# Second pass of the attention scores: low part of k on both halves, 128 rows instead of 64

## The chip, the cores and the metric

One core of a Trainium2 chip runs the whole forward pass of a two-layer decoder trunk in one launch. The metric is device time in microseconds. The kernel before took 1227.51 us (median of 3 runs, 1226.98 to 1227.97). Five engines work side by side, each through its own queue in order: TensorE (PE in the profile, its weight loads PEld), VectorE (DVE), ScalarE (ACT), GpSimd (POOL) and SyncE (SP, which here issues the DMAs).

## The reference, cut to what matters

Sequence 512, width 1024, two layers. Each layer multiplies the normed input by one weight matrix whose columns are q, k, v and two branches of a recurrent block. The attention has 4 heads, and each head has two components of 64 dimensions:

```
s = einsum('bqhcd,bkhcd->bhcqk', q_blk, k) * scale      # c: two components, d: 64
s = where(causal mask, s, -inf)
pr = softmax(s)
attn = pr[:, :, 0] - lam * pr[:, :, 1]
out = attn @ v
```

After it come a norm of each head, the recurrent block (convolution, gates, scan), one output projection, an MLP with squared ReLU, and a gated embedding per layer. All is float32.

## The kernel before

Every tensor lies with features on the 128 partitions and the 512 tokens along the columns. TensorE multiplies in a format that keeps fewer bits than float32, so each operand is split into a high part (rounded by a ScalarE copy) and a low part (what is left, by a VectorE subtraction). A product of two tensors is then three passes: high by high, high by low, low by high. The weights come in chunks of 128x1024 by DMA (`raw`) and are split into `wh` and `wl`.

The two components of a head share one tile of 128 rows, 64 rows each. `rope_done` rotates q or k (it ends in `t1`) and splits it. For q it makes one tile per component, `x0` and `x1`: on the component's own 64 rows the high part, on the other 64 rows the low part. For k it makes `y0` and `y1`, the high part of a component on both halves, and one tile `lo` that holds the low part of component 0 in rows 0 to 63 and of component 1 in rows 64 to 127.

`unit_scores` then needs three passes for a block of 128 queries and one component, into one PSUM bank:

- the first has `q[c]` as stationary operand and `k[c]` as moving one, all 128 rows: high by high on one half, low by high on the other, summed in one pass;
- the second takes the high part of q and the low part of k, on the component's own 64 rows alone;
- the third adds the causal mask to the last 128 columns, an identity times a mask tile (`identr`, `maskr`), 128 rows.

Block qi has (qi + 1) x 128 columns, so the passes are 128, 256, 384 or 512 columns wide. There are 4 blocks x 2 components x 4 heads x 2 layers = 64 such triples. `unit_max` takes the maxima and exponentials, `unit_mix` mixes the two components, `unit_T` transposes and `head_av` multiplies by v.

All instructions are recorded first, through an object (`Plan`) that stands in for the engines. A list scheduler then sets the order of every engine at once: it takes what is ready by its own costs, oldest first with some boosts, within a window of 600 instructions. So dense products of the next head stand between the passes of a head's scores. Tiles of 128x512 come from one pool of 57 (`T`), score banks from 6 PSUM banks (`PM`), of which scores hold 4 at most. The profile puts every instruction on line 182, the line that issues them, so the tiles' names tell them apart: `sc` is a score bank, `ky` the high part of k, `kl` its low part, `qx` a q tile, `dense` the bank of a projection, `up` of the MLP's first product.

Of the kernel before, what the change touches and what calls it, by code (L numbers as in the profile page):

```python
# [21 lines left out]
KD = D // 128  # L22
# [3 lines left out]
NQ = KF // KD  # L26
ORDER = (0, 4, 1, 5, 2, 6, 3, 7)     # output tiles, so that the halves of the features that Strassen pairs come together
HS = S // 2
# [4 lines left out]

# buffers
TB = 57     # tiles of [128, 512]
AT = 2      # tiles for the probabilities of a head, transposed
RAW = 4     # weight chunks as loaded
WB = 6      # weight chunks, split
SC = 4      # PSUM banks that scores may hold

# chunks split ahead in the MLP's products
UA = 2
DA = 2

# the list schedule
WIN = 600   # instructions beyond the oldest one not issued that it may choose from
EV = 150    # boost of what frees PSUM
LP = 600    # how far the norm's sums are put off
RE = -50    # boost of the rotary tables
SW = 2      # us that an instruction waits at most for others that need no new activation table  # L50
SF = 8      # free tiles from which on no check for deadlock is needed
WU = 8      # products that warm up the tensor engine
NM = 4      # output tile of the first up product after which the norm's scale is computed

# [11 lines left out]
class Plan:  # L66
    """Records instructions and issues them in the order of a list schedule: each engine takes, of what is ready,
    what was recorded first (less its boost)."""

# [114 lines left out]
    def schedule(self):  # L184
# [36 lines left out]
        def safe(i):  # L221
            """Whether all that is older than the newest instruction issued can still find its tiles in program order."""
            need = {}
# [132 lines left out]

# columns of the packed per-feature vectors
VCOL = {}
# [16 lines left out]
def chunk_list():  # L375
    """Weight chunks of [128, 1024] in the order in which they are used."""
    c = []
    for l in range(DEPTH):
        c += [("in", l, 12 + m) for m in range(2)]
        c += [("gates", l, 0)]  # L380
        c += [("in", l, 12 + m) for m in range(2, 4)]
        c += [("v", l, i) for i in range(4)]
        for h in range(NH):
            c += [("in", l, h), ("in", l, 4 + h)]
        c += [("in", l, 16 + m) for m in range(4)]
        c += [("out", l, m) for m in ORDER]
        for q in range(NQ):
            c += [("up", l, q * KD + m) for m in range(KD)]
            c += [("down", l, m, q) for m in ORDER]
        c += [("proj", l, 0)]  # L390
        c += [("gate", l, m) for m in range(4)]
        c += [("proj", l, 1)]
        c += [("gate", l, m) for m in range(4, 8)]
    return c
# [6 lines left out]
def build(ctx: ExitStack, tc: tile.TileContext, given, x, p, pos, w, vec, lamqk, out):  # L401
# [25 lines left out]

    # ---------------- weights: streamed, split into two parts that add up exactly
    raw_t, w_t = {}, {}
# [3 lines left out]
    def w_half(i, c):  # L433
        """Half a chunk, for the products that come first."""
        t, hi, lo = T("w0"), T("w0h", F32R), T("w0l", F32R)
# [30 lines left out]
    def pair_parts(a1, a2):  # L466
        """The seven weight operands of Strassen's product (Winograd's form) for two output tiles."""
        lft, rgt = slice(0, S), slice(S, 2 * S)
# [37 lines left out]
    def split(src, hi, lo):  # L506
        """src (SBUF or PSUM) into hi + lo."""
        act(out=hi, in_=src, func=AF.Copy)
        ve.tensor_tensor(out=lo, in0=src, in1=hi.bitcast(F32), op=ALU.subtract)
# [8 lines left out]

    # ---------------- constants
    vt = const.tile([128, NV], F32, name="vt")  # L520
# [21 lines left out]
    def warm_up():  # L542
        """Products of zeros that bring the tensor engine to its full clock while the first loads run."""
        z = T("z", F32R)
# [15 lines left out]
    def rope_setup():  # L560
        """cos and signed sin of the angles, feature-major, 1 and 0 on the rows that don't rotate."""
        posf = T("posf")[:, 0:NT]
# [6 lines left out]
        NA = NT * 16  # L569
        # ang = hi + lo, 1/(2 pi) as a sum of 12-bit parts: every product is exact  # L570
        rest, parts = 1.0 / (2.0 * math.pi), []
# [58 lines left out]
    def vec_setup():  # L630
        for l in range(DEPTH):
            act(out=hb[:, l, 0:4], in_=vt[:, VCOL["b_gate_a", l]:VCOL["b_gate_a", l] + 4], func=AF.Copy, scale=0.5)
            act(out=hb[:, l, 4:8], in_=vt[:, VCOL["b_gate_x", l]:VCOL["b_gate_x", l] + 4], func=AF.Copy, scale=0.5)
            act(out=gsub[:, l:l + 1], in_=V("g_subln", l), func=AF.Copy, scale=1.0 - lam_init(l))
        # softplus(-x) = max(-x, 0) + log1p(exp(-|x|)), the log1p as 2 atanh(y / (2 + y))
        n = DEPTH * 4
# [18 lines left out]
        ve.tensor_scalar(out=sp4n.rearrange("p l t -> p (l t)"), in0=s, scalar1=-4.0, scalar2=None, op0=ALU.mult)  # L655
        # lambda of the differential attention, on every partition
        lq = T("lq")
# [11 lines left out]

    # ---------------- norms: h times its gain goes into the products, 1/rms after them  # L670
    class Norm:
# [20 lines left out]
        def stats(self, square=False):  # L692
            """1/rms (or its square), token-major, and spread over the partitions."""
            ps = PS("msq")
# [24 lines left out]
    class FinalNorm:  # L719
        """The last norm, on each half of the tokens as soon as that is complete."""  # L720

# [35 lines left out]
    def group(ws, rhs, nk, done, late=0, mid=None, tk=slice(0, S)):  # L757
        """ws: per output tile a function giving the chunk slices of K tile k. The last `late` K tiles come last."""
        pss_ = [PM("dense") for _ in ws]
# [16 lines left out]

    # ---------------- one layer
    def layer(l, h, nm, last):
        hg = lambda k: nm.hg[k]
        gate_w = [None]  # L780
        scan_o = [None] * 4
        yo = [None] * KD     # 0..3 attention heads, 4..7 recurrent tiles

# [4 lines left out]

        # recurrent branch
        lru = [dict() for _ in range(4)]  # L790
# [68 lines left out]

        # x branch  # L860
        ws = [take_in(12), take_in(13)]
# [8 lines left out]

        # v, token-major
        pv = [PM("pv") for _ in range(NT)]
# [19 lines left out]

        # attention
        mask_sh = [(i ^ 8) if i < 16 else i for i in range(32)]

        def rope_done(ps, dst):
# [6 lines left out]
            if not dst:  # L903
                # q: per component, its hi part on its own rows and its lo part on the other's
                x0, x1 = T("qx", F32R), T("qx", F32R)
# [5 lines left out]
            else:  # L911
                # k: per component, its hi part on both, and its lo part on its own rows
                y0, y1, lo = T("ky", F32R), T("ky", F32R), T("kl", F32R)
                for y, src in ((y0, t1[ca, :]), (y1, t1[cb, :])):
                    act(out=y[ca, :], in_=src, func=AF.Copy)
                    act(out=y[cb, :], in_=src, func=AF.Copy)
                for y, c in ((y0, ca), (y1, cb)):
                    ve.tensor_tensor(out=lo[c, :], in0=t1[c, :], in1=y[c, :].bitcast(F32), op=ALU.subtract)
                dst.append((y0, y1, lo))

        att, s0_ = {}, {}

        def unit_scores(hd, qi, q, k):
# [4 lines left out]
            for c in range(2):  # L928
                pc = slice(64 * c, 64 * c + 64)
                ps = PM("sc")  # L930
                mm(ps[:, 0:n], lhsT=q[c][:, qs], rhs=k[c][:, 0:n], start=True, stop=False)
                mm(ps[:, 0:n], lhsT=q[c][pc, qs], rhs=k[2][pc, 0:n], start=False, stop=False)
                mm(ps[:, qs], lhsT=identr, rhs=maskr, start=False, stop=True)
# [95 lines left out]

        # gate branch  # L1030
        for t in range(4):
            group([take_in(16 + t)], hg, KD, lambda i, ps: gr_done(t, ps))

        # output projection; the recurrent tiles come first, the last head last
        order = [4, 5, 6, 7, 0, 1, 2, 3]

        nm2 = Norm("g_mlp", l)
        bp = [dict() for _ in range(4)]     # Strassen's operands of h times its gain, per pair of feature tiles
        fp, t4s = [None] * KD, []
        fat = [AT, []]  # L1040

        def BT(name):
            """512 columns of a tile like those that hold a head's probabilities, as long as there are any."""
            if not fat[1] and fat[0]:
# [40 lines left out]

        # MLP in quarters of the hidden features; the first product by Strassen's method over pairs of output tiles,
        # halves of the input features and halves of the tokens
        nm3 = Norm("g_ple", l)
# [73 lines left out]

        # per-layer embedding
        nmn = None if last else Norm("g_mix", l + 1)
# [18 lines left out]
        def ple(ms, ws, tk, done, **kw):  # L1183
            """proj and gate products of the output tiles ms on the tokens tk."""
            pj = []
# [93 lines left out]
def _layout(i):  # L1279
    """Lays the arrays out as the launch reads them."""  # L1280
    a = {k: np.asarray(v) for k, v in i.items()}
# [59 lines left out]
```

## Time and profile before

| what | value |
|---|---|
| median of 3 runs | 1227.51 us |
| span of the profiled execution | 1225.4 us |
| PE busy | 1210.8 us (99%) |
| PEld busy | 1049.7 us (86%) |
| DVE busy | 949.0 us (77%) |
| ACT busy | 654.8 us (53%) |
| POOL busy | 21.4 us (2%) |
| mean DMA rate | 94 GB/s |

The span runs from the first to the last instruction of the execution that was profiled; the time of a run holds a little more than that. Busy times of an engine are unions of its instructions' durations. Those of PE overlap, since a product starts before the one ahead has drained: the distance between two starts tells what a pass costs the stream, and its duration is longer.

### The profile page before, as it was taken

To read this page: it belongs to the slowest core of one execution; us is meant where nothing else is said; L and a number is where in the kernel's file an instruction comes from. 1 tells how busy PE (TensorE), PEld (TensorE's weight loads), DVE (VectorE), ACT (ScalarE), POOL (GpSimd) and SP (SyncE) were. 2 spreads that over 40 slices of the span, in tenths; PEclk is the share of its full clock that TensorE was granted. 3 is DMA by queue.
4 is the path that set the end of the run, shared out by engine and by line. 5 is a ranking of instruction groups with operands and counts; after the bars stand their busy time and mean duration, and the time that the engine had idled before them with its cause. 6 is when DMAs were issued, how large, how long until landed. Compare 5 with 4: busy or idle time off the path is not lost.

```text
span 1225.4 us, 17658 instructions
## 1 busy us (share of the span) xinstructions
PE 1210.8 (99%) x6848; PEld 1049.7 (86%) x6848; DVE 949.0 (77%) x1642; ACT 654.8 (53%) x1068; POOL 21.4 (2%) x43
## 2 busy tenths in 40 slices
PE   8999999999999999999999999999999999999996
PEld 6877788998988989988888777889899899898886
DVE  9898889987777678575778888799776787786564
ACT  6875557743543535543458566576445354355352
POOL 1000000000000000000000000000000000000000
PEclk9999999999999999999999999999999999999998
DMA  6321133243332333332323111223433333343202
GB/s 234 103 69 52 52 89 101 85 124 100 106 103 90 118 93 114 103 103 87 104 69 118 55 35 52 75 81 107 134 103 104 91 104 97 91 136 103 86 1 69
DMA packets 34371, 114.71 MB, mean 94 GB/s; under 512 B 3952, under 2 KB 6000, under 8 KB 34288
## 3 DMA queue, kind: packets, MB, share of 16 engines
q1 hardware_dynamic: 34288, 113.59, 30.2%
q8 instruction: 54, 0.88, 0.3%
q14 instruction: 29, 0.24, 0.1%
HBM read 111.48 MB, written 2.10 MB: 93 GB/s over the span
## 4 chain that ended last, share of the span: by engine, by line
PE 94%; DVE 3%; ACT 1%; DMA 0%; issue 0%; POOL 0%; SPq 0%; POOLq 0%; DVEq 0%; ACTq 0%
PE dense L182 55%; PE up L182 26%; PE sc L182 4%; PE pv L182 2%; PE pj L182 2%; PE av L182 1%; PE bc L182 1%; PE tr L182 1%; PE msq L182 1%; PE osm L182 0%; PE gates L182 0%; DMA h<-x 0%; DVE hs L182 0%; DVE a L182 0%; ACT ky L182 0%
## 5 line engine op out<-in xcount | busy, mean ns | idle before, releaser
L182 ACT ACTIVATE wh<-raw 128x1024 fp32r<-128x1024 f32 x204 | 214.3, 1057 | 279.6 <-PE dense L182 151.8
L182 DVE TENSOR_TENSOR wl<-raw,wh 128x1024 fp32r<-128x1024 f32 x204 | 247.6, 1218 | 22.4 <-ACT wh L182 22.0
L182 PE MATMUL dense<-ffh,wh 128*128 128x512 f32 x512 | 199.5, 390 | 0.0
L182 PE MATMUL dense<-ffl,wh 128*128 128x512 f32 x512 | 199.4, 389 | 0.0
L182 PE MATMUL dense<-ffh,wl 128*128 128x512 f32 x512 | 199.2, 389 | 0.0
L182 PE MATMUL dense<-hgh,wl 128*128 128x512 f32 (+1 forms) x400 | 151.3, 378 | 0.0
L182 PE MATMUL dense<-hgh,wh 128*128 128x512 f32 (+1 forms) x400 | 151.1, 378 | 0.0
L182 PE MATMUL dense<-hgl,wh 128*128 128x512 f32 (+1 forms) x400 | 150.3, 376 | 0.0
L182 PEld LDWEIGHTS dense<-ffh,wl 128*128 128x128 f32 x512 | 96.1, 188 | 20.0
L182 PEld LDWEIGHTS dense<-ffh,wh 128*128 128x128 f32 x512 | 96.1, 188 | 19.8
L182 PEld LDWEIGHTS dense<-ffl,wh 128*128 128x128 f32 x512 | 96.2, 188 | 19.5
L182 ACT ACTIVATE sh<-s 128x512 fp32r<-128x512 f32 x96 | 59.9, 628 | 78.1 <-DVE s L182 77.6
L182 DVE TENSOR_TENSOR dn<-dense,rbc 128x512 f32<-128x512 f32 x64 | 44.2, 690 | 72.7 <-PE dense L182 71.9
L182 PE MATMUL up<-bl,wh 128*128 128x256 f32 x352 | 99.6, 283 | 0.0
L182 PE MATMUL up<-bh,wl 128*128 128x256 f32 x352 | 99.6, 283 | 0.0
L182 PE MATMUL up<-bh,wh 128*128 128x256 f32 x352 | 99.5, 283 | 0.0
L182 PEld LDWEIGHTS dense<-hgl,wh 128*128 128x128 f32 x400 | 75.5, 189 | 12.1
L182 PEld LDWEIGHTS dense<-hgh,wl 128*128 128x128 f32 x400 | 75.5, 189 | 11.9
L182 PEld LDWEIGHTS dense<-hgh,wh 128*128 128x128 f32 x400 | 75.5, 189 | 11.8
L182 PE MATMUL up<-bl,sh 128*128 128x256 f32 x288 | 81.5, 283 | 0.0
L182 PE MATMUL up<-bh,sl 128*128 128x256 f32 x288 | 81.5, 283 | 0.0
L182 PE MATMUL up<-bh,sh 128*128 128x256 f32 x288 | 81.3, 283 | 0.0
(236 smaller groups left out, 2572.0 us busy)
## 6 DMA issues: line engine op xcount, KB each, us to landing
raw<-w SPq DMA_DIRECT2D x204, 512.0 KB, 3.6
h<-x SPq DMA_DIRECT2D x8, 256.0 KB, 5.4
out<-fin SPq DMA_DIRECT2D x8, 256.0 KB, 2.4
w<-w SPq DMA_DIRECT2D x4, 256.0 KB, 4.5
pT<-p SPq DMA_DIRECT2D x4, 256.0 KB, 4.0
lq<-lamqk SPq DMA_DIRECT2D x1, 256.0 KB, 7.1
vt<-vec SPq DMA_DIRECT2D x1, 61.0 KB, 2.4
posi<-pos SPq DMA_DIRECT2D x1, 2.0 KB, 3.0
```

The lines of the kernel that those rows point to most:

```text
L182: d["fn"](*d["args"], **d["kw"])
```

## The change

For k, each component now has a low tile of its own, `los[0]` and `los[1]`. The subtraction writes the component's own half as before, and a ScalarE copy writes the same values into the other half. The second pass of the scores uses all 128 rows of `q[c]` and of that tile. It so adds the low part of q times the low part of k, which was left out before.

```diff
             else:
-                # k: per component, its hi part on both, and its lo part on its own rows
-                y0, y1, lo = T("ky", F32R), T("ky", F32R), T("kl", F32R)
-                for y, src in ((y0, t1[ca, :]), (y1, t1[cb, :])):
+
+                ys, los = [T("ky", F32R), T("ky", F32R)], [T("kl", F32R), T("kl", F32R)]
+                for y, src in zip(ys, (t1[ca, :], t1[cb, :])):
                     act(out=y[ca, :], in_=src, func=AF.Copy)
                     act(out=y[cb, :], in_=src, func=AF.Copy)
-                for y, c in ((y0, ca), (y1, cb)):
+                for y, lo, c, o in zip(ys, los, (ca, cb), (cb, ca)):
                     ve.tensor_tensor(out=lo[c, :], in0=t1[c, :], in1=y[c, :].bitcast(F32), op=ALU.subtract)
-                dst.append((y0, y1, lo))
+                    act(out=lo[o, :], in_=lo[c, :].bitcast(F32), func=AF.Copy)
+                dst.append((ys, los))
...
             for c in range(2):
-                pc = slice(64 * c, 64 * c + 64)
                 ps = PM("sc")
-                mm(ps[:, 0:n], lhsT=q[c][:, qs], rhs=k[c][:, 0:n], start=True, stop=False)
-                mm(ps[:, 0:n], lhsT=q[c][pc, qs], rhs=k[2][pc, 0:n], start=False, stop=False)
+                mm(ps[:, 0:n], lhsT=q[c][:, qs], rhs=k[0][c][:, 0:n], start=True, stop=False)
+                mm(ps[:, 0:n], lhsT=q[c][:, qs], rhs=k[1][c][:, 0:n], start=False, stop=False)
                 mm(ps[:, qs], lhsT=identr, rhs=maskr, start=False, stop=True)
                 d["ps"].append(ps)
```

The other lines of the diff only take comments out.

## Rows read from the trace of the kernel before

**Rows 1.** The page, part 4: the chain that ended last, share by engine.

```profile
PE 94%; DVE 3%; ACT 1%; DMA 0%; issue 0%; POOL 0%; SPq 0%; POOLq 0%; DVEq 0%; ACTq 0%
```

**Rows 2.** Windows: us, busy us and count by engine, granted clock, DMA share, GB/s.

```profile
80.00:186.00 106.00, 104.86 (x509) 80.92 (x508) 89.56 (x204) 61.38 (x136) 5.55 (x4) 1.00 0.23 70
186.00:217.00 31.00, 31.00 (x139) 25.64 (x138) 30.33 (x52) 23.23 (x38) 0.00 (x0) 1.00 0.28 86
...
680.00:783.00 103.00, 102.40 (x499) 79.28 (x499) 88.41 (x205) 61.40 (x136) 6.63 (x4) 1.00 0.18 52
```

**Rows 3.** Timeline of PE: start us, duration us, tiles, form, count.

```profile
84.10 0.39 PE L182 MATMUL dense<-hgh,wl 128*128 128x512 f32 x1
84.42 0.32 PE L182 MATMUL sc<-kl,qx 64*128 64x128 f32 x1
84.67 0.33 PE L182 MATMUL sc<-maskr,identr 128*128 128x128 f32 x1
84.93 0.32 PE L182 MATMUL sc<-kl,qx 64*128 64x128 f32 x1
...
91.40 0.28 PE L182 MATMUL sc<-ky,qx 128*128 128x256 f32 x1
91.61 0.38 PE L182 MATMUL sc<-kl,qx 64*128 64x256 f32 x1
91.92 0.33 PE L182 MATMUL sc<-maskr,identr 128*128 128x128 f32 x1
92.08 0.39 PE L182 MATMUL sc<-ky,qx 128*128 128x384 f32 x1
...
96.33 0.42 PE L182 MATMUL sc<-ky,qx 128*128 128x512 f32 x1
96.68 0.49 PE L182 MATMUL sc<-kl,qx 64*128 64x512 f32 x1
97.10 0.33 PE L182 MATMUL sc<-maskr,identr 128*128 128x128 f32 x1
97.26 0.45 PE L182 MATMUL sc<-ky,qx 128*128 128x512 f32 x1
```

**Rows 4.** The tile `sc`: second passes, durations min/median/max in ns, their forms.

```profile
L182 PE MATMUL sc<-kl,qx x64: 322/409/502, 84.4 to 759.2; 64*128 64x128 f32 x16, 64*128 64x256 f32 x16, 64*128 64x384 f32 x16, 64*128 64x512 f32 x16
```

**Rows 5.** Chain in order of time: start us, us, what, passes.

```profile
162.70 0.89 PE bc L182 x8
...
185.78 31.99 PE dense L182 x141
217.77 40.31 PE up L182 x336
```

**Rows 6.** Timeline of the weight loads, same columns as the PE timeline.

```profile
83.87 0.19 PEld L182 LDWEIGHTS dense<-hgh,wl 128*128 128x128 f32 x1
84.41 0.18 PEld L182 LDWEIGHTS sc<-kl,qx 64*128 64x128 f32 x1 [0.36 <-issue]
84.67 0.19 PEld L182 LDWEIGHTS sc<-maskr,identr 128*128 128x128 f32 x1
```

**Rows 7.** ACT by form: count, busy us, mean ns, idle before.

```profile
L182 ACT ACTIVATE wh<-raw 128x1024 fp32r<-128x1024 f32 x204 | 214.3, 1057 | 279.6 <-PE dense L182 151.8 <-issue 52.2 <-PE up L182 51.2
...
L182 ACT ACTIVATE ky<-q 64x512 fp32r<-64x512 f32 x32 | 20.1, 628 | 7.3 <-DVE q L182 6.9
```

**Rows 8.** Timeline of DVE: second subtraction of a head's k.

```profile
83.18 0.69 DVE L182 TENSOR_TENSOR kl<-q,ky 64x512 fp32r<-64x512 f32 x1
```

**Rows 9.** Waits of DVE, 80 to 186 us: total us, times, longest.

```profile
DVE at L182 <- ACT at L182: 5.8, 9, 1.1
DVE ome L182 <- PE osm L182: 3.0, 3, 1.4
DVE mx L182 <- PE sc L182: 1.7, 3, 0.8
DVE o L182 <- PE bc L182: 1.4, 3, 0.7
```

## The prediction, on record before the changed kernel ran

> **What bounds the kernel now.** I read the page first. The span is 1225.4 us, and the chain of work that ended last runs through TensorE for 94% of it [rows 1]. The kernel is a TensorE stream, so what is taken off that stream shortens the time as long as no other engine takes over. The second look is the windows by stage: the attention stages, which hold all the code that changes, are 80 to 186 us in layer 0 and 680 to 783 us in layer 1. There TensorE is busy 104.86 of 106 us and 102.40 of 103 us at a granted clock of 1.00, VectorE 89.56 and 88.41, ScalarE about 61 in each [rows 2]. TensorE is the bound there too, with VectorE second at 84 to 86%. In the output projection that follows, VectorE is busy 30.33 of 31 us without holding TensorE up, so it can run nearly full [rows 2].
>
> But a busy TensorE is not one at its rate. The third look is its timeline, where I take the distance from one start to the next, not the durations. An undisturbed stream needs 31.99 / 141 = 0.227 us for a pass of 512 columns, 40.31 / 336 = 0.120 us for 256 and 0.89 / 8 = 0.111 us for 128 [rows 5]. The scores do not keep that. The triple of 512 columns (high part of k, low part, mask) starts at 96.33, 96.68 and 97.10, and the next pass at 97.26: 0.35 + 0.42 + 0.16 = 0.93 us, where 0.227 + 0.227 + 0.111 = 0.565 would do [rows 3]. All three are stretched: the pass ahead of the 64-row one, the 64-row one itself (most), and the one behind it. The weight loads show why. The load of a full-row dense pass starts at 83.87 and its product at 84.10, so it lies 0.23 us ahead, under the pass before. The load of the 64-row pass starts at 84.41 and its product at 84.42: nothing of it is hidden [rows 3, 6]. Each step from 128 rows to 64 and back lets the array run empty first.
>
> **The change, part by part.** *The second pass on all rows.* There are 64 such passes, 16 of each width, and each stands alone between 128-row passes, so each pays both steps [rows 3, 4]. Excess of a triple: 512 columns 0.93 - 0.565 = 0.365 us. 256 columns: 91.40 to 92.08 is 0.68 us against 2 x 0.120 + 0.111 = 0.351, so 0.33. 384 columns: between these two, 0.35, an interpolation. 128 columns: low part and mask start at 84.42 and 84.67 and the next low part at 84.93, 0.51 us against 2 x 0.111 = 0.22, so 0.29 [rows 3, 5]. The sum is 16 x (0.29 + 0.33 + 0.35 + 0.365) = 21.4 us of TensorE time, half of it in each layer. Columns and count of passes stay the same. That a 64-row pass costs no less than a full one in the array itself is why I charge nothing for the added rows: even here its distance is above that of the full-row pass beside it (0.42 against 0.35) [rows 3].
>
> A rule that would speak against this stands in the Trainium skill, TensorE: Matmul & The Clock Gate, Part 3: a weight load runs under a product in flight only when the two use different row groups. By that rule the full-row load would wait as well, and the sum would be 0. This case's trace does not agree for full-row passes: the load at 83.87 lies 0.23 us ahead of its product while another full-row product runs [rows 3, 6].
>
> *Two added copies per head.* The low part of k now goes to the other half as well: 2 ScalarE copies of 64x512 per head, 16 in all. The copies of k's high part have that form and last 628 ns [rows 7], so this is 16 x 0.63 = 10.1 us, 5 us per layer, on an engine that is idle for more than 40 us of each attention stage [rows 2]. Hidden by the dense products of the next head, which the planner puts into TensorE's queue meanwhile. Without that cover it would be at most 2 x 0.63 = 1.3 us per head, 10 us in all. What is queued behind on ScalarE are weight splits and exponentials, each 0.6 us later per copy, and TensorE and VectorE wait for those.
>
> *The longer way to the second pass.* The subtraction that makes the low part ends at 83.18 + 0.69 = 83.87, and the first pass that reads it starts at 84.42 [rows 3, 8]. That 0.55 us does not hold a copy of 0.63 us with its two hand-overs, so the pass has to come later, and the planner, which knows the copy's cost, will put a few more dense products ahead of it. I take 0. Bounds: 0, and about 0.5 us for each of 8 heads, 4 us.
>
> *One more tile of low parts per head* out of the pool of 57, and the count of VectorE subtractions (2 per head) unchanged: 0. The order written out is made anew, so neighbours may swap. I allow 2 us either way, about the 1.14 + 0.60 us that TensorE idles in the two stages now [rows 2].
>
> *What is late next.* With 10.7 us off each stage, VectorE's 89.56 us stand in some 95. Its volume fits, but its order is fixed too. Of its listed waits in layer 0, those for TensorE (3.0 + 1.7 + 1.4 = 6.1 us) shrink when TensorE is quicker; those for ScalarE (5.8 us) do not [rows 9]. If nothing else of VectorE's idle time gave way, the two layers would gain 2 x 6.1 = 12.2 us only, layer 1 taken like layer 0. So the gain lies between 12.2 and 21.4 us. TensorE's idle time is small now, which puts me near the upper end: I let its 1.74 us of idle time triple, 3.5 us more, and get 21.4 - 3.5 = 18 us.
>
> The profiled span is 1225.4 us and the median of the runs 1227.51, 2.1 us more, which I carry over. Span after: 1225.4 - 18 = 1207.4; forecast 1209.5 us.
>
> **The rivals.** *VectorE's order holds the stage.* Then 12.2 us are gained: 1215. For it: 84 to 86% busy already, and waits for ScalarE that stay. Against it: 98% in the next stage with TensorE unhindered [rows 2].
>
> *The drain does not go with the row count.* If the stretched starts came from the change of operand (another slice of q, the mask's weights) and not from the rows, or if a full-row load waited as the rule above says, the time would stay at 1227.5. Against it: all loads of full-row dense passes run ahead, and the load behind the 64-row pass, a full-row one, is late only there [rows 3, 6].
>
> *Slower: the copy is the last link of the second pass.* ScalarE takes its queue in order. If in each head both copies stood behind two weight splits (1.057 us each), TensorE, which also takes its queue in order, would wait 2 x 1.057 + 2 x 0.628 = 3.4 us per head, 27 us in all, against 21.4 saved: 1227.5 + 5.6 = 1233. It decides from 21.4 / 8 = 2.7 us of wait per head. Against it: dense products are at hand in nearly every head, and the planner issues ScalarE's work by what is due.
>
> **How the numbers follow.** About 0.2% (2.5 us) is what a measurement here tells from no change. Forecast, with its own range 1203 to 1213 us: chance 0.66. VectorE's order: 0.24, 1213 to 1222. No drain to save: 0.05, of which a tenth would be chance movement below or above the bound. Copy on the path: 0.05, of which a fifth ends within the bound. So faster 0.91, same 0.05, slower 0.04. The range 1203 to 1221 leaves out about 0.16: the last two cases, and the ends of the first two. Its lower end is the full 21.4 us, the 2 us of a luckier order and 1 us of the runs' own spread (1226.98 to 1227.97); its upper end lies beyond the gain of 12.2 us by the 4 us of a late second pass and the 2 us of an unlucky order.
>
> **What would show it.** The second pass appears with 128 rows and a distance to the next start of about 0.23 us at 512 columns, its weight load some 0.2 us ahead of it, and the mask's pass falls from 0.16 to about 0.11. A triple of 512 columns takes 0.57 us. The attention stages are 9 us shorter each, all other stages within 1 us of before, and VectorE's share in them is above 90%. ScalarE shows 16 new copies of 64x512. The prediction is wrong if the triples shrink and the stages do not (then the waits of TensorE in them grew by as much), or if the triples keep their 0.9 us.

## The result, and the profile after

The changed kernel takes 1206.52 us (median of 4 runs, 1206.03 to 1207.2) against 1227.74 us for the kernel before, measured beside it. The ratio is 0.9828, with a 95% interval of 0.9814 to 0.9842. It is 21.2 us faster; the forecast was 18 us.

The stages of the kernel after, in windows (columns as in [rows 2]). The first is layer 0's attention, the second layer 1's:

```profile
80.00:174.00 94.00, 92.24 (x499) 77.15 (x498) 88.53 (x205) 65.87 (x144) 5.78 (x4) 1.00 0.24 76
670.50:761.50 91.00, 90.81 (x496) 77.30 (x496) 84.94 (x200) 65.50 (x143) 4.78 (x4) 1.00 0.19 59
```

TensorE does the same kind of work in 94 and 91 us that took 106 and 103. These windows hold a few passes less than before (499 and 496 against 509 and 499), so they show a little too much of a gain. VectorE's busy time fell by only 1.0 and 3.5 us, so its share rose from 84 to 94% in layer 0 and from 86 to 93% in layer 1. ScalarE gained 4.5 and 4.1 us, with the added copies in it. The chain in order of time tells where each layer's MLP starts, which closes the account of the stages. Of before (layer 0 stands in [rows 5], at 217.77):

```profile
817.32 38.99 PE up L182 x325
```

and of after:

```profile
208.31 38.99 PE up L182 x325
796.46 38.99 PE up L182 x325
```

Layer 0 gains 217.77 - 208.31 = 9.5 us, layer 1 another 817.32 - 796.46 - 9.5 = 11.4 us. Nothing else gains (the span is 20.2 us shorter, so what follows gives 0.7 us back): a whole quarter of the MLP's second product takes 43.55 us for its 192 passes in both kernels, here in after:

```profile
334.29 43.55 PE dense L182 x192
```

The triples themselves, in TensorE's timeline of after, against [rows 3]:

```profile
83.55 0.39 PE L182 MATMUL dense<-hgh,wl 128*128 128x512 f32 x1
83.78 0.22 PE L182 MATMUL sc<-kl,qx 128*128 128x128 f32 x1
83.84 0.28 PE L182 MATMUL sc<-maskr,identr 128*128 128x128 f32 x1
83.96 0.33 PE L182 MATMUL sc<-kl,qx 128*128 128x256 f32 x1
...
93.84 0.27 PE L182 MATMUL sc<-ky,qx 128*128 128x256 f32 x1
93.95 0.28 PE L182 MATMUL sc<-kl,qx 128*128 128x256 f32 x1
94.07 0.22 PE L182 MATMUL sc<-maskr,identr 128*128 128x128 f32 x1
94.13 0.39 PE L182 MATMUL sc<-ky,qx 128*128 128x384 f32 x1
...
99.34 0.40 PE L182 MATMUL sc<-ky,qx 128*128 128x512 f32 x1
99.58 0.40 PE L182 MATMUL sc<-kl,qx 128*128 128x512 f32 x1
99.81 0.22 PE L182 MATMUL sc<-maskr,identr 128*128 128x128 f32 x1
99.88 0.44 PE L182 MATMUL sc<-ky,qx 128*128 128x512 f32 x1
```

The triple of 512 columns went from 0.93 to 0.54 us (99.34 to 99.88), that of 256 from 0.68 to 0.29, and low part with mask at 128 columns from 0.51 to 0.18 (this is the triple of [rows 3]; for most of the 16 of this width it is 0.42 before and 0.22 after). The second pass now starts the next one 0.23 us later at 512 columns. Its weight load, in the timeline of the loads, is ahead of it again, where [rows 6] had it at the product's own start:

```profile
83.56 0.19 PEld L182 LDWEIGHTS sc<-kl,qx 128*128 128x128 f32 x1
83.79 0.19 PEld L182 LDWEIGHTS sc<-maskr,identr 128*128 128x128 f32 x1
```

The load at 83.56 belongs to the product at 83.78, 0.22 us later. Over the whole trace of before, the loads of the scores were held up 77 times where the profile shows nothing that they waited for (total us, times, longest):

```profile
PEld sc L182 <- issue: 17.7, 77, 0.4
```

After has no such row. The added copies are there, by form (columns as in [rows 7]):

```profile
L182 ACT ACTIVATE kl<-kl 64x512 fp32r<-64x512 f32 x16 | 10.1, 630 | 0.8 <-DVE kl L182 0.4
```

### The profile page after: what moved, and what is told of

It reads as the page before. It is cut to its first block, busy times and chain, and to the rows that moved or that the text cites. A ratio compares the mean times of both kernels' runs of the same rounds, so it can differ in the third digit from the quotient of the medians.

```text
span 1205.2 us, 17677 instructions
## 1 busy us (share of the span) xinstructions
PE 1191.3 (99%) x6848; PEld 1048.2 (87%) x6848; DVE 947.6 (79%) x1642; ACT 664.3 (55%) x1084; POOL 19.8 (2%) x43
## 4 chain that ended last, share of the span: by engine, by line
PE 91%; DVE 5%; ACT 2%; issue 0%; DMA 0%; SPq 0%; POOLq 0%; DVEq 0%; ACTq 0%
PE dense L182 54%; PE up L182 27%; PE pv L182 2%; PE pj L182 2%; PE sc L182 2%; PE bc L182 1%; PE av L182 1%; DVE qr L182 1%; PE tr L182 1%; PE msq L182 1%; DVE wl L182 1%; DVE q L182 1%; PE osm L182 0%; PE gates L182 0%; DMA h<-x 0%
```

## The experiments

The theory: each stay on 64 rows between full-row passes has a price on TensorE, and the change saves 64 of them. The rivals: the gain came from the order that the planner made anew; or the stretch belongs to the operands or the waits of the attention and not to the rows. In the first four experiments the queues hold the same instructions in the same order as those of the kernel to compare with, so that the row count alone differs. (Where the planner would have chosen another order, its cost model is given 128 rows for every pass.)

### The changed kernel with its second pass back on 64 rows

```diff
-                mm(ps[:, 0:n], lhsT=q[c][:, qs], rhs=k[1][c][:, 0:n], start=False, stop=False)
+                pc = slice(64 * c, 64 * c + 64)
+                mm(ps[:, 0:n], lhsT=q[c][pc, qs], rhs=k[1][c][pc, 0:n], start=False, stop=False)
```

Expected:

> The changed kernel with every instruction and every queue's order as it is there, the copies of the low part included, but the second pass of the scores back on the 64 rows of its own component. Theory (the step from 128 rows to 64 and back is what costs): the triples of 512 columns take 0.93 us again instead of 0.54, and the time goes back by 20 to 24 us, to 1226 to 1230 us. Rival (the gain came from the order that the planner made anew): stays at 1206 to 1208 us.

Measured: 1226.38 us, inside the 1226 to 1230 us expected and 19.9 us above the changed kernel, at the lower edge of the 20 to 24 us. It is 0.999 of before (0.9981 to 1.0). The triples are stretched as they were, here those of 256 and 384 columns in its timeline:

```profile
94.54 0.38 PE L182 MATMUL sc<-kl,qx 64*128 64x256 f32 x1
94.85 0.33 PE L182 MATMUL sc<-maskr,identr 128*128 128x128 f32 x1
95.02 0.39 PE L182 MATMUL sc<-ky,qx 128*128 128x384 f32 x1
```

The second pass takes 0.31 us to the next start and the mask 0.17. The row of the held-up loads is back as well:

```profile
PEld sc L182 <- issue: 17.1, 71, 0.4
```

So the new order and the copies together are worth about 1 us (1227.54 against 1226.38) while the second pass is on 64 rows, which is hardly told from nothing; the row count is worth the rest. The rival of the order falls.

### The kernel before on 128 rows, without copies

```diff
-                mm(ps[:, 0:n], lhsT=q[c][pc, qs], rhs=k[2][pc, 0:n], start=False, stop=False)
+                mm(ps[:, 0:n], lhsT=q[c][:, qs], rhs=k[2][:, 0:n], start=False, stop=False)
```

Expected:

> The kernel before with its own order of every queue and without any copy; only the second pass now runs over all 128 rows of the one tile of low parts. It adds to each score the low part of q times the low part of the other component's k, a term that the reference does not have. Theory: 20 to 24 us faster than before, 1204 to 1208 us, and within 2 us of the changed kernel, since the copies lie beside other work. Rival (the 16 copies of 0.63 us stand in the way): 3 to 10 us below the changed kernel, 1197 to 1203 us. Rival (the new order gave the gain): 1227 us.

Measured: 1206.01 us (1205.69 to 1206.88), ratio to before 0.9826 (0.9812 to 0.9841). The old order gives the whole gain with full rows. The changed kernel is 0.5 us above it, and the ranges of the two overlap. Since their orders differ, this bounds only copies and order together; what the copies cost by themselves is not shown.

### Pairs of 64-row passes, and the same order on 128 rows

```diff
+            for c in range(2):
+                mm(pss2[c][:, 0:n], lhsT=q[c][:, qs], rhs=k[c][:, 0:n], start=True, stop=False)
+            for c in range(2):
+                pc = slice(64 * c, 64 * c + 64)
+                with first(100000 * c):
+                    mm(pss2[c][:, 0:n], lhsT=q[c][pc, qs], rhs=k[2][pc, 0:n], start=False, stop=False)
+            for c in range(2):
+                mm(pss2[c][:, qs], lhsT=identr, rhs=maskr, start=False, stop=True)
...
+            for i, j in ((2, 1), (3, 2), (4, 3), (5, 3)):     # so that the planner keeps them together
+                nc.nodes[at_ + i]["deps"].add(at_ + j)
```

The yardstick has `q[c][:, qs]` and `k[2][:, 0:n]` in the second pass and is otherwise the same. Expected of the pairs:

> The kernel before with both components' second passes, still on 64 rows each, one straight behind the other (32 pairs in place of 64 single ones), in an order of its own that the run beside it shares. Theory (the price is per stay on 64 rows, not per pass): slower than the run beside it by half of 24, 10 to 13 us; if the two passes, which use different halves of the rows, also run at the same time, by 5 to 8 us only. Rival (the price is per 64-row pass): slower by 20 to 24 us.

and of the yardstick:

> The same order as the run with the pairs, instruction by instruction, with both second passes on all 128 rows of the one tile of low parts (the term of the other component is added to the scores as in the run without copies). It is the yardstick for the pairs. Theory: like the run without copies but for what the order costs, 1204 to 1212 us.

Measured: pairs 1209.95 us (1209.84 to 1210.34), yardstick 1204.08 us (1203.81 to 1204.36). The difference is 5.9 us, inside the 5 to 8 us of passes that run at the same time; a price for each 64-row pass would have given 20 to 24. The timeline of the pairs:

```profile
94.23 0.28 PE L182 MATMUL sc<-ky,qx 128*128 128x256 f32 x1
94.43 0.39 PE L182 MATMUL sc<-kl,qx 64*128 64x256 f32 x2
94.75 0.44 PE L182 MATMUL sc<-maskr,identr 128*128 128x128 f32 x2
95.03 0.39 PE L182 MATMUL sc<-ky,qx 128*128 128x384 f32 x1
95.34 0.44 PE L182 MATMUL sc<-kl,qx 64*128 64x384 f32 x2
95.71 0.44 PE L182 MATMUL sc<-maskr,identr 128*128 128x128 f32 x2
95.99 0.45 PE L182 MATMUL dense<-hgl,wh 128*128 128x512 f32 x1
```

and of its yardstick at the same places:

```profile
93.54 0.28 PE L182 MATMUL sc<-ky,qx 128*128 128x256 f32 x1
93.65 0.40 PE L182 MATMUL sc<-kl,qx 128*128 128x256 f32 x2
93.89 0.33 PE L182 MATMUL sc<-maskr,identr 128*128 128x128 f32 x2
94.06 0.39 PE L182 MATMUL sc<-ky,qx 128*128 128x384 f32 x1
94.29 0.52 PE L182 MATMUL sc<-kl,qx 128*128 128x384 f32 x2
94.64 0.33 PE L182 MATMUL sc<-maskr,identr 128*128 128x128 f32 x2
94.81 0.45 PE L182 MATMUL dense<-hgl,wh 128*128 128x512 f32 x1
```

Two passes of 64x256 together take 0.32 us to the next start (94.43 to 94.75), as one alone does (0.31 in the first experiment): in the trace of all 32 pairs the second starts 0.003 to 0.004 us after the first. Two of 128x256 take 0.24 us one after the other. At 256 columns the stretch from the first row to the next triple is 0.80 us against 0.52, so a stay costs 0.28 us more than it saves; the pass that it saves is worth 0.12, so the stay itself costs 0.40 us. At 384 columns it is 0.96 - 0.75 = 0.21, with 0.175 for the saved pass 0.385 us. The Trainium skill, TensorE: Matmul & The Clock Gate, Part 3, states that products on different row groups run at the same time; in this pair the trace agrees. In the kernel before no two 64-row passes ever stood side by side, so it paid a stay for each and had nothing back.

### The price of a stay where nothing waits

```diff
+                    if half and k == 3:
...
+                        mm(pss_[i][:, tk], lhsT=wl[0:64, :], rhs=rh[0:64, tk], start=False, stop=False)
```

Expected:

> The changed kernel, order of every queue unchanged, with 64 passes elsewhere cut to 64 rows: in the MLP's second product, of each output tile's fourth K tile, the pass of the weights' low part takes rows 0 to 63 alone (the other half of that small term is left out). TensorE never waits in that stage, so nothing can hide or absorb the price. Theory: each such stay costs what the triples of 512 columns showed, 0.35 to 0.39 us over its three passes, 64 x 0.37 = 24 us: 1229 to 1232 us. Rival (the stretch belongs to the attention, its operands or its waits): less than 5 us, 1206 to 1211 us.

Measured: 1232.08 us (1231.7 to 1232.43), 25.6 us above the changed kernel, 0.40 us for each of 64 stays. That is a little over the expected 0.35 to 0.39 and just past the 1229 to 1232 us. TensorE's timeline around one:

```profile
252.61 0.39 PE L182 MATMUL dense<-ffl,wh 128*128 128x512 f32 x1
252.93 0.49 PE L182 MATMUL dense<-ffh,wl 64*128 64x512 f32 x1
253.35 0.50 PE L182 MATMUL dense<-ffh,wh 128*128 128x512 f32 x1
253.69 0.40 PE L182 MATMUL dense<-ffl,wh 128*128 128x512 f32 x1
```

and its loads:

```profile
252.38 0.19 PEld L182 LDWEIGHTS dense<-ffl,wh 128*128 128x128 f32 x1
252.93 0.18 PEld L182 LDWEIGHTS dense<-ffh,wl 64*128 64x128 f32 x1 [0.36 <-issue]
253.35 0.19 PEld L182 LDWEIGHTS dense<-ffh,wh 128*128 128x128 f32 x1 [0.24 <-issue]
```

The three distances are 0.32, 0.42 and 0.34 us where 0.227 each would do: 0.09 on the way in, 0.19 for the pass itself, 0.11 behind it, 0.40 in all. Both loads at the steps start with their products. The quarter's 192 passes, 8 stays among them, show the same sum:

```profile
337.56 46.75 PE dense L182 x192
```

It is 46.75 - 43.55 = 3.2 us longer, 0.40 per stay. So the stretch does not belong to the attention, and the rival of operands and waits falls.

### Pairs in the changed kernel, and the copies on GpSimd

The changed kernel in the order of the pairs, with its copies, so that no term is left out or added:

```diff
-                mm(ps[:, 0:n], lhsT=q[c][:, qs], rhs=k[1][c][:, 0:n], start=False, stop=False)
...
+            for c in range(2):
+                with first(100000 * c):
+                    mm(pss2[c][:, 0:n], lhsT=q[c][:, qs], rhs=k[1][c][:, 0:n], start=False, stop=False)
```

Expected:

> The changed kernel with both components' passes of a block one straight behind the other (high parts, then both low parts, then both masks), low parts copied to both halves, so nothing is left out or added. The run with one shared tile of low parts in such an order took 1204.1 us. Theory (TensorE's waits set what is left, and the pair order shortens them): 1203 to 1206 us. Rival (the copies cost something in this order, where the second passes come together): 1206 to 1210 us.

Measured: 1207.49 us (1205.84 to 1208.41), in the rival's range and 3.4 us above the yardstick without copies. What TensorE's score loads wait for there:

```profile
PEld sc L182 <- ACT pr L182: 3.9, 8, 0.9
...
PEld sc L182 <- ACT kl L182: 0.6, 2, 0.4
```

and in the yardstick:

```profile
PEld sc L182 <- ACT pr L182: 1.9, 9, 0.4
```

They wait 3.9 us for exponentials (which free score banks) against 1.9 us, and 0.6 us for the copies themselves. That pointed at ScalarE, so the copies went to GpSimd in both orders:

```diff
-                    act(out=lo[o, :], in_=lo[c, :].bitcast(F32), func=AF.Copy)
+                    nc.gpsimd.tensor_copy(out=lo[o, :], in_=lo[c, :].bitcast(F32))
```

Expected of the pairs with it:

> The run with pairs and copies, with the 16 copies on GpSimd, which is idle for 98% of the span, in place of ScalarE; the planner makes the order anew. Theory (the 10 us of copies on ScalarE delay the exponentials that free the score banks): back to the level of the pairs without copies, 1203 to 1206 us. Rival (the copy's place at the end of the chain to the second pass costs, on whichever engine): 1206 to 1210 us, more if GpSimd's copy is slow.

and of the changed kernel with it:

> The changed kernel with the copies on GpSimd. Theory (ScalarE is not the bound in the changed kernel's own order, as the run without copies is only 0.5 us faster): within 2 us of the changed kernel, 1205 to 1208 us. Rival (ScalarE's work costs here too): 1202 to 1205 us.

Measured: 1206.14 us (1205.23 to 1206.66) and 1208.06 us (1207.67 to 1209.02). The pairs gain 1.4 us, but the ranges overlap and the result lies where the two expectations meet; the changed kernel loses 1.5 us, just past the 1205 to 1208 us expected, and the intervals of the two ratios to before overlap (0.9828 to 0.9855 against 0.9814 to 0.9842). The score loads' waits for exponentials hardly changed: 3.6 us against 3.9 in the pairs, 3.2 against 3.3 in the changed kernel. So it is not shown that the copies on ScalarE caused them. Each time the whole order was made anew. With the place of the copies, and the order with it, the time moved by some 1.5 us in either direction; which of the two does it stays open.

The quickest of all is the yardstick of the pairs, 1204.08 us, 0.9809 of before (0.9793 to 0.9826): full rows, one shared tile of low parts, no copies, and the term of the other component added. With every term as in the changed kernel, none is clearly below it.

## Why the prediction was right

*The price of the steps between 128 and 64 rows.* Right in mechanism, and shown by the runs with unchanged order: 64 rows in the new kernel give the time back, 128 rows in the old one give the gain. The sum was put at 21.4 us. With the triples of after shown above as the yardstick it is 16 x (0.33 + 0.39 + 0.39 + 0.39) = 24.0 us, 384 columns taken between its neighbours as before. The starts of all 64 triples in the traces give less: 22.7 us between before and its order on 128 rows, 21.5 us between the changed kernel and its order on 64. So the sum was right to about 1 us, and that closely by some luck. The undisturbed mask was put too dear: I took 0.111 us from a stream of 128-column passes, and behind 256 columns or more it costs 0.06 to 0.07 (99.81 to 99.88, 94.07 to 94.13), which is 48 x 0.05 = 2.4 us. And the 0.29 us at 128 columns came from a triple whose mask is followed by another 64-row pass at once. In 12 of the 16 it is not, and there the mask takes 0.16 us and not 0.26; the step into the 64-row pass, 0.09 us, which I left out at this width, happens to make up for it.

*The rule that a load waits for products on the same rows.* It would have given 0. The load at 83.56, 0.22 us ahead of its product among full-row passes, and the 21 us say otherwise.

*The copies hidden.* Right for the changed kernel: 16 copies of 630 ns, 10 us of ScalarE, and TensorE's score loads wait for one of them only:

```profile
PEld sc L182 <- ACT kl L182: 0.4, 1, 0.4
```

In the order of the pairs 0.6 us of waiting shows, and the rest is open as told.

*What is lost to waits.* This is the term that was mis-sized. I allowed 3.5 us, TensorE's idle time in the two stages tripled. It hardly grew: 1.74 us before, 1.76 + 0.19 = 1.95 us after. Between the runs of the same order, 1.3 us (order of before) and 1.9 us (order of the changed kernel) of what the triples gained came back elsewhere in the starts of these two stages. So the allowance was about 2 us too large, the larger part of the 3.2 us by which the forecast fell short. One wait did grow, here in after:

```profile
PEld sc L182 <- ACT pr L182: 3.3, 8, 1.1
```

The score loads wait 3.3 us for exponentials, 8 times, against 1.4 us in before. In the same order with 64 rows it is almost gone:

```profile
PEld sc L182 <- ACT pr L182: 0.3, 1, 0.3
```

So it is the quicker stream that meets this wait, and not the new order. A load that waits need not hold TensorE up as long: 3.0 us more of this wait stand beside the 1.9 us that came back.

*VectorE's order.* That rival would have given 1215. VectorE's share reached 94 and 93%, above the 90% named, without becoming the bound; its waits for ScalarE shrank too, from 5.8 us in [rows 9] to these in layer 0's attention after, 2.0 us:

```profile
DVE at L182 <- ACT at L182: 1.1, 2, 0.6
DVE s L182 <- ACT pr L182: 0.9, 3, 0.5
```

I had taken them as fixed. *The copy on the path* (1233) did not come, though not in the way that I expected. In layer 0's first head the planner put 6 dense products, and not 9, between the first high pass and the first low one. It brought the second subtraction forward instead, from 83.18 [rows 8] to right behind the first, and both copies follow (VectorE and ScalarE of after):

```profile
82.01 1.40 DVE L182 TENSOR_TENSOR kl<-q,ky 64x512 fp32r<-64x512 f32 x2
82.72 1.35 ACT L182 ACTIVATE kl<-kl 64x512 fp32r<-64x512 f32 x2 [0.36 <-DVE kl L182]
```

In each of the 8 heads the last copy ended before the first low pass began, by 0.05 to 1.95 us.

## What to carry to other kernels

Read TensorE's rate from the distance between starts and from how far a weight load lies ahead of its product; a busy share of 99% hid some 22 us here. A matmul on half the rows, alone among full-row ones, was dearer here than a full one by about 0.4 us, so fill the other half, with a copy that an idle engine makes or, where the result allows it, with a small term that happens to lie there. If half-row passes are wanted, put those of different halves side by side. One such pair in a stay did not pay for it (32 pairs were 5.9 us slower than full rows); longer stays were not tried.

## What the runs showed of the hardware that was not expected

- The price of a stay on 64 rows is the same in the attention (0.385 to 0.40 us by the pairs) and in an undisturbed stream (0.40 us), at 256, 384 and 512 columns. The Trainium skill, TensorEngine Tiling (Array Packing), Tiling Modes, says that a change of mode drains TensorE; the trace agrees, in that the loads at both steps start only with their own products, and adds the size.
- A 128-column pass behind one of 256 to 512 columns and ahead of another long one takes 0.06 us to the next start, against 0.111 us in a run of such passes. In the triples of 128 columns, where the pass ahead is as short as the mask, it takes 0.11 us too.
- Two 64-row passes on different halves and different banks, side by side, take 0.32 us to the next start together at 256 columns, one alone 0.31.
